# Where the token sums and six branch weights are made: out of the first projection and the SGU stage, into the two merges

## The chip, the cores and the metric

The kernel runs on one core of one Trainium2 chip. The metric is the device time of one execution in microseconds (us). Engines are named as in the profile: PE is the TensorE matmul unit (PEld its weight load), DVE the vector engine, ACT the scalar engine, POOL the GpSimd engine and SP the engine that only issues transfers. "L161" is line 161 of the kernel's file. A matrix in two parts, a high and a low half in f16, is multiplied by three f16 matmuls, which is how the kernel keeps f32 accuracy on PE.

## The reference

One layer of a hybrid token mixer is computed for 2048 sample tokens and 128 prompt tokens (`DEPTH = 1`, `D_MODEL = 1024`):

```python
xn = rmsnorm(h, ln_g) * (1 + scale) + shift
proj = einsum('btd,de->bte', xn, w_in)          # one input projection for all branches
qkv, beta, dec, z_a, u_b, v_b, z_b, x_c, z_c, gates = split(proj)
...
o_a = rmsnorm(delta_bidir(short_conv(qkv), g, beta)) * silu(z_a)     # gated DeltaNet, forward and backward
o_b = chunk_sgu(u_b, v_b, ...) * silu(z_b)                           # spatial gating
o_c = fourier_mix(x_c, grid) * silu(z_c)
pb = einsum('btnw,nwd->btnd', stack([o_a, o_b, o_c]), w_branch)
merged = einsum('btnd,btnd->btd', sigmoid(gates), pb)                # three merge gates
out = einsum('btd,de->bte', merged, w_out)
y = rmsnorm(h + gate * out)
```

The gates of the last merged branch (branch A, n = 0) need `xn` times a 1024 x 1024 block of `w_in`. For the sample tokens the kernel makes this product with seven block products in place of eight (a Strassen scheme), whose right-hand sides are sums and differences of blocks of `xn`: these are the *token sums*.

## The kernel before

The normalised tokens lie in SBUF for nearly the whole run as four f16 tiles `x00, x01, x10, x11` (first or second 1024 tokens, first or second half of the channels) in two parts each, with `xp` for the prompt tokens. The work passes through these stages, in program order:

- **Start** (to about 165 us): modulation, norm, transposes, and the z_a gates.
- **qkv** (about 165 to 490 us, L767 to L807): twelve column panels `ct` of 128 channels. A panel is five blocks of tokens (`TBS`: four of 512, one of 128); each block is 24 matmuls (8 k-slices by three parts, `gemm_T`), and ACT copies it to `raw` (L784). Then DVE runs the short convolution over the whole row of 2178 (L793 to L795), ACT a sigmoid, POOL the product (L799).
- **SGU** (about 490 to 614 us): the v projection, 17 chunks of tokens.
- u, z_b, x_c, z_c with the Fourier mixing (to about 1136 us).
- **First merge** `merge(1, ...)` (1136 to 1470) and **second merge** `merge(2, ...)` (1470 to 1807): eight column blocks `db`, each in two halves of the tokens (`HALVES`: two blocks, then three). A block is a gate product (24 matmuls), a sigmoid on ACT into an `sg` tile (L1530), a branch product (12 matmuls), and a multiplication on DVE (L1536, or L1539 with an addition on POOL, L1540).
- **Last merge** with the seven products, and the **output** projection (1807 to 2240).

Beside the panels runs a second strand of work, cut into small steps by `yield` and stepped by `pace.tick` as the panels advance: first the decay factors (`decays()`, in the qkv stage), then the preparation and the scan of the DeltaNet (`delta()`, from the SGU stage to the end of the second merge). A third strand converts weights: SP reads a block of weights into one of two `wst` tiles, ACT squares it (L209), DVE narrows the sum (`wscb`, L175), PE adds it over the partitions in one matmul with `ones`, DVE makes a power of two of it (`wsc`, L183 to L187, and `winv`, L220), ACT writes the high half (`whi`, L222) and DVE the low half (`wlo`, L223). `wlist` holds the order of all weights. Weights that are needed much later (`early`: eight blocks of `w_out`, eight of `w_branch` for branch A) are converted ahead and put into DRAM by `keep_next(i)`; each of them costs the whole chain, one factor on DVE (`oinv`, L752, or `b0inv`, L750) and two stores issued by ACT.

The token sums are a generator of 32 steps, `token_sums()` (L701): eight groups (two token halves by four k-slices) of four steps, each of which makes one 128 x 512 sum or difference, splits it into two f16 parts and stores it to DRAM (`sD`, printed as `xs`). The POOL part adds the two halves of x to an f32 tile `sg` (L717, four a group), makes one difference (L727) and one low part (L709); DVE makes three sums or differences (L723, L730, L734) and three low parts (L709); ACT makes four high parts (L708); POOL issues the four stores (L711, and L738 for the last two of all). A group holds `sg` tiles (four in all, shared with the gate sigmoids of the merges) and `st` tiles (three in all).

The order in which each engine takes its instructions is not the program's order: a scheduler replays the program with a model of durations, picks for each engine the ready instruction of the highest priority, and writes the result down. On the chip each engine then takes its list strictly in that order. `tc.high_priority()` raises an instruction in that choice; `tc.issue_after(ins)` puts instructions behind a named one.

Before the change, twelve steps of the sums are taken in the first three panels of qkv (one beside each block of 512 tokens, L786), the other twenty behind the last store of the decay factors (L804). Ten `early` weights are converted in the SGU stage (L1351), six in the second half of the qkv stage (L790).

Of the kernel before, what the change touches and what calls it, by code (L numbers as in the profile page):

```python
# [20 lines left out]
P = 128  # L21
D = 1024
KT = 8
# [88 lines left out]
def hybrid_flow_kernel(ctx: ExitStack, tc: tile.TileContext, x_prompt, x_sample, state_delta, c, c_ctx, ln_g, w_ada,  # L112
# [151 lines left out]
    wlist = []  # L264
# [4 lines left out]
    for i in range(12):  # L269
        wlist.append((w_in_[:, C_QKV + i * P:C_QKV + (i + 1) * P], KT, "w", 4))  # L270
        if i > 5:
            wlist.append(early[i - 6])
    wlist += [(w_in_[:, C_V + g * P:C_V + (g + 1) * P], KT, "v", 4) for g in range(4)] + early[6:]
    for c0 in [x_ + g * P for g in range(4) for x_ in (C_U, C_ZB)] + [x_ + g * P for g in range(4) for x_ in (C_XC, C_ZC)]:
        wlist.append((w_in_[:, c0:c0 + P], KT, "w", 4))
    gw_ = lambda n, db: w_in_[:, C_G + n * D + db * P:C_G + n * D + (db + 1) * P]
    bw_ = lambda n, db: (w_branch[0, n][:, db * P:(db + 1) * P], 4, "b", 2)
    for n in (1, 2):
        for db in range(KT):
            wlist += [(gw_(n, db), KT, "w", 4), bw_(n, db)]  # L280
    for j in range(4):
        wlist += [(gw_(0, j), KT, "w", 4), (gw_(0, 4 + j), 4, ("t2", j), 4)]
    for kind in ("t1", "t3"):
# [234 lines left out]
    for ti, (t0, tn) in enumerate(TBS):  # L518
        if t0 not in xts:
            load_x(t0, tn)  # L520
        g = 0 if t0 < NS else 1
# [235 lines left out]
    def keep_next(i):  # L757
        if 0 <= i < 8:
            keep([oD[l][:, i, :] for l in range(2)], oinv[:, i:i + 1], sx)
        elif 8 <= i < 16:  # L760
            keep([bD[l][i - 8] for l in range(2)], b0inv[:, i - 8:i - 7])
        elif i == 16:
            flush_kept()
# [7 lines left out]
    for ct in range(12):  # L771
        w = getw(1, 3 if ct < 6 else min(5, 16 - ct))
        for half in range(1):
            raw = sb(a1p, [P, LP], "raw")
            G.memset(raw[:, 0:1], 0.0)
            G.memset(raw[:, NS + 1:NS + 3], 0.0)
            G.memset(raw[:, LP - 1:LP], 0.0)
            for t0, tn in TBS:
                flip[0] ^= 1
                ps = bank(ps_d if flip[0] else ps_mm, [P, tn])  # L780
                gemm_T(ps, w, x_all(t0, tn))
                o = t0 + 1 if t0 < NS else t0 + 3
                with tc.high_priority():
                    A.activation(raw[:, o:o + tn], ps, AF.Copy, scale=w.inv)  # L784
                pace.tick(tn / 100)
                if ct < 3 and tn == 512:  # L786
                    next(sums)
                if ct > 4:
                    weight_step()
                if ct > 5 and t0 == 1024:  # L790
                    keep_next(ct - 6)
            y = sb(a1p, [P, LP - 2], "cy")
            V.tensor_scalar(y, raw[:, 0:LP - 2], convw(0, ct), None, ALU.mult)  # L793
            V.scalar_tensor_tensor(y, raw[:, 1:LP - 1], convw(1, ct), y, ALU.mult, ALU.add)
            V.scalar_tensor_tensor(y, raw[:, 2:LP], convw(2, ct), y, ALU.mult, ALU.add)  # L795
            for c0 in range(0, LP - 2, CQ):
                c1 = min(c0 + CQ, LP - 2)
                A.activation(raw[:, 1 + c0:1 + c1], y[:, c0:c1], AF.Sigmoid)  # L798
                G.tensor_tensor(y[:, c0:c1], y[:, c0:c1], raw[:, 1 + c0:1 + c1], ALU.mult)  # L799
            G.dma_start(qkvD[ct], y)  # L800
            if ct < 4 or ct > 7:
                A.activation(raw[:, 1:LP - 1], y, AF.Square, accum_out=vqs[:, ct:ct + 1])
    wsn = sb(ep, [P, WB], "st", bufs=3).rearrange("p (g q) -> p g q", g=4)
    SY.dma_start(wsn, w_spatial[0].rearrange("g p q -> p g q"))  # L804
    pace.drain()
    with tc.issue_after(dlast[0].ins):
        for _ in sums:  # L807
            pass
    a1.close()


# [517 lines left out]
    for t in range(NCH):  # L1329
# [18 lines left out]
        if t == 8:  # L1348
            SY.dma_start(cf, consts[:, _CF:_CW])
        weight_step()  # L1350
        if t % 3 != 1:  # L1351
            keep_next(6 + 2 * (t // 3) + (t % 3) // 2)
        pace.tick(5.2)
    spatial(*vprev)
    while vout:
# [147 lines left out]
    def merge(n, first, inv, each=None, halves=HALVES, mid=None, then=None):  # L1503

        steps, sinv = iter(()), None
        for db in range(KT):
# [8 lines left out]
            for h0, hn, tbs in halves:  # L1515
# [2 lines left out]
                    SY.dma_start(mrow, mD[db][:, h0:h0 + hn])  # L1518
                if each is not None and (n == 0 or db > 3):
                    next(gates, 0)  # L1520
                for t0, tn in tbs:
                    if first and db == 0:
                        for tb in TBS[0:2] if t0 == 0 else TBS[TBS.index((t0, tn)) + 1:][:1]:
# [55 lines left out]
            pace.drain()  # L1579

    inv_ = merge(2, False, inv_, finish_delta, then=(0, 17))
    cs_.close()


# [259 lines left out]
```

## Time and profile before

| what | value |
|---|---|
| median of three runs | 2239.32 us (2233.18 to 2240.04) |
| the profiled execution | 2242.02 us |
| its span, first to last instruction | 2240.2 us |
| mean granted clock of PE | 0.984 |
| PE busy | 2134.1 us, 95% of the span |
| DVE busy | 1443.1 us, 64% |
| ACT busy | 1047.8 us, 47% |
| POOL busy | 827.7 us, 37% |
| transfers | 404.94 MB, 181 GB/s on average |

The span is the profiled execution's own time without what lies around it (1.8 us). The profile gives, for each engine, its busy time, the idle time before each instruction and the event that ended it. Since every engine takes its list in order, an engine that idles before an instruction holds up everything behind it. PE is busy 95% of the span, so the time is what PE does plus the 106 us in which it does nothing, plus what it loses where its granted clock is below 1.

### The profile page before, as it was taken

How to read it: one execution, taken by the hardware profiler on the slowest of the kernel's cores; microseconds unless marked ns; L12 is line 12 of the kernel's file. 1: busy time of each engine (PE TensorE's matmuls, PEld its weight loads, DVE VectorE, ACT ScalarE, POOL GpSimd, SP SyncE). 2: the span in 40 equal slices, each digit the busy share in tenths (PEclk: the TensorE clock that was granted, in tenths of full speed). 3: DMA queues.
4: the chain of work that ended last, by engine and by line, in shares of the span. 5: the costliest groups of instructions: out<-in, count | busy, mean ns of one | idle time of the engine just before them, and what ended most of it. 6: DMA issues, size and time to landing. Idle time of an engine off the chain costs nothing. (4 is left out here: it accounts for less than half of the span.)

```text
span 2240.2 us, 42450 instructions
## 1 busy us (share of the span) xinstructions
PE 2134.1 (95%) x15878; PEld 1227.4 (55%) x15878; DVE 1443.1 (64%) x3250; ACT 1047.8 (47%) x2394; POOL 827.7 (37%) x972
## 2 busy tenths in 40 slices
PE   7998978999899999899999999999999999999998
PEld 3564433445555567788755565565555445444443
DVE  5748989558888877735565555675565455444553
ACT  3634754546565656334464444665554332222331
POOL 1445467322243332233312232345453323433443
PEclk9999989999999999999999999999999999999999
DMA  8423944448787765424475555676664856564542
GB/s 273 159 83 119 313 158 148 145 134 253 230 289 227 215 199 154 106 83 143 130 223 172 161 167 175 201 231 207 202 204 153 255 165 201 179 223 149 167 142 86
DMA packets 333625, 404.94 MB, mean 181 GB/s; under 512 B 41345, under 2 KB 240106, under 8 KB 330602
## 3 DMA queue, kind: packets, MB, share of 16 engines
q1 hardware_dynamic: 311114, 327.36, 48.1%
q0 software_dynamic: 15248, 59.66, 7.3%
q10 hardware_dynamic: 7056, 15.21, 1.8%
q8 instruction: 125, 2.05, 0.4%
q14 instruction: 82, 0.67, 0.1%
HBM read 259.83 MB, written 142.30 MB: 180 GB/s over the span
## 5 line engine op out<-in xcount | busy, mean ns | idle before, releaser
L161 PE MATMUL b<-x,whi 128*128 128x512 f16 x3008 | 908.2, 382 | 5.5 <-DVE sg L1539 2.5
L161 PE MATMUL b<-x,wlo 128*128 128x512 f16 x1504 | 574.2, 382 | 0.0
L161 PEld LDWEIGHTS <-whi 128*128 128x128 f16 x3776 | 346.5, 98 | 338.1 <-issue 35.6
L161 PEld LDWEIGHTS <-wlo 128*128 128x128 f16 x1888 | 185.6, 98 | 180.7 <-issue 13.8
L161 PE MATMUL b<-big,bhi 128*128 128x512 f16 (+1 forms) x960 | 251.7, 348 | 2.9 <-ACT big L1500 1.5
L161 PE MATMUL b<-big,blo 128*128 128x512 f16 (+1 forms) x480 | 163.4, 348 | 0.0
L161 PEld LDWEIGHTS <-x 128*128 128x128 f16 x2176 | 131.3, 98 | 43.6 <-issue 4.2
L161 PEld LDWEIGHTS <-bhi 128*128 128x128 f16 x960 | 86.8, 98 | 74.9 <-issue 3.7
L161 PE MATMUL b<-x,m 128*128 128x512 f16 x528 | 114.8, 379 | 0.0
L799 POOL TENSOR_TENSOR cy<-cy,raw 128x545 f32<-128x545 f32 (+1 forms) x48 | 72.4, 1547 | 109.6 <-ACT raw L798 109.6
L1022 POOL COPY T<-ES 32x256 f16<-32x256 f16 x68 | 31.4, 462 | 208.1 <-DMA ES<-ei 202.5
L209 ACT ACTIVATE wlo<-wst 128x1024 f16<-128x1024 f32 (+1 forms) x64 | 64.2, 1003 | 93.6 <-DMA wst<-in_w_in_dram 64.0
L223 DVE SCALAR_TENSOR_TENSOR wlo<-wst,wsc,whi 128x1024 f16<-128x1024 f32 (+1 forms) x64 | 91.1, 1426 | 19.3 <-ACT whi L222 18.8
L222 ACT ACTIVATE whi<-wst,wsc 128x1024 f16<-128x1024 f32 (+1 forms) x64 | 69.7, 1093 | 64.2 <-DVE wsc L186 57.9
L161 PE MATMUL b<-whi,x 128*128 128x128 f16 x1024 | 90.7, 219 | 0.0
L1128 POOL TENSOR_TENSOR skn<-skn,ed 128x512 f32<-128x512 f32 x34 | 36.3, 1067 | 144.8 <-DMA skn<-kv 128.5
L175 DVE CAST wscb<-wss 128x1 bf16<-128x1 f32 x101 | 15.3, 152 | 111.9 <-ACT wlo L209 74.3
L161 PE MATMUL b<-wlo,x 128*128 128x128 f16 x512 | 87.4, 219 | 0.0
L161 PEld LDWEIGHTS <-m 128*128 128x128 f16 x528 | 51.1, 98 | 61.4
L161 PE MATMUL b<-x,zhi 128*128 128x512 f16 x256 | 78.7, 383 | 0.1
L161 PE MATMUL b<-v4hi,x 128*128 128x512 f16 x256 | 78.5, 383 | 0.1
L1660 POOL TENSOR_TENSOR mrow<-mrow,sg 128x512 f32<-128x512 f32 (+1 forms) x40 | 46.5, 1165 | 82.2 <-DVE sg L1659 73.9
(483 smaller groups left out, 4475.6 us busy)
## 6 DMA issues: line engine op xcount, KB each, us to landing
wst<-in_w_in_dram SPq DMA_DIRECT2D x56, 512.0 KB, 4.7
qkv<-cy POOLq DMA_DIRECT2D x12, 1089.0 KB, 5.7
st<-br SPq DMA_DIRECT2D x48, 256.0 KB, 3.5
mrow<-mrg SPq DMA_DIRECT2D x16, 576.0 KB, 4.5
mrg<-mrow POOLq DMA_DIRECT2D x16, 576.0 KB, 3.7
dc<-dec SPq DMA_DIRECT2D x17, 512.0 KB, 4.6
kq<-qkv SPq DMA_DIRECT2D x34, 256.0 KB, 4.2
kv<-tok POOLq DMA_DIRECT2D x17, 512.0 KB, 5.6
```

What stands on the lines that cost most here:

```text
L161: PE.matmul(out, l, r, start=start, stop=stop)
L175: V.tensor_copy(sb16, ss)
L209: A.activation(w.lo, st, AF.Square, accum_out=ss)
L222: w.made = A.activation(w.hi, st, AF.Copy, scale=s)
L223: V.scalar_tensor_tensor(w.lo, st, s, w.hi, ALU.mult, ALU.subtract)
L799: G.tensor_tensor(y[:, c0:c1], y[:, c0:c1], raw[:, 1 + c0:1 + c1], ALU.mult)
L1022: G.tensor_copy(T16[rows(a0, b), :, :, b], ES[0:32, :, 2 * a0 + b, :, wT])
L1128: G.tensor_tensor(h3(kn_), h3(kn_), bc(ed[:, d, t, :], P), ALU.mult)
L1660: G.tensor_tensor(mr, mr, sg, ALU.add)
```

## The change

The sums are taken out of the qkv stage altogether. They are made in the first two merges, in the second half (`h0` not zero) of the column blocks 1 to 4: one group of four steps each time, four groups in the first merge and four in the second. Whatever is left of the generator (the last two stores) is run after the second merge.

Of the `early` weights, six (branch weights 2 to 7 of branch A) are no longer converted in the SGU stage but in the first merge, one in each of the column blocks 1 to 6, beside the second half; the seventh call there stores the last one. In the SGU stage four are left (two of `w_out`, two of `w_branch`), taken at every fourth chunk.

```diff
@@ wlist @@
-    wlist += [(w_in_[:, C_V + g * P:C_V + (g + 1) * P], KT, "v", 4) for g in range(4)] + early[6:]
+    wlist += [(w_in_[:, C_V + g * P:C_V + (g + 1) * P], KT, "v", 4) for g in range(4)] + early[6:10]
...
     for n in (1, 2):
         for db in range(KT):
-            wlist += [(gw_(n, db), KT, "w", 4), bw_(n, db)]
+            wlist += [(gw_(n, db), KT, "w", 4), bw_(n, db)] + early[9 + db:10 + db if n == 1 and db else 0]
@@ qkv stage @@
                 pace.tick(tn / 100)
-                if ct < 3 and tn == 512:
-                    next(sums)
                 if ct > 4:
                     weight_step()
...
     pace.drain()
-    with tc.issue_after(dlast[0].ins):
-        for _ in sums:
-            pass
     a1.close()
@@ SGU stage @@
         weight_step()
-        if t % 3 != 1:
-            keep_next(6 + 2 * (t // 3) + (t % 3) // 2)
+        if t % 4 == 3:
+            keep_next(6 + t // 4)
         pace.tick(5.2)
@@ merge @@
                 if each is not None and (n == 0 or db > 3):
                     next(gates, 0)
+                if h0 and db and n == 1:
+                    keep_next(9 + db)
+                if h0 and 0 < db < 5:
+                    for _ in range(4):
+                        next(sums)
                 for t0, tn in tbs:
@@ after the second merge @@
     inv_ = merge(2, False, inv_, finish_delta, then=(0, 17))
+    for _ in sums:
+        pass
     cs_.close()
```

The scheduler makes new lists of it. Three places of them follow.

**DVE, early in the qkv stage**, where the decay factors are computed (tile `tok`; L584 to L610 is one dependent chain, of which PE waits for the end). The difference of the two lists:

```order
 L598 RECIPROCAL tok_1779<-tok_1779 128x136
-L730 TENSOR_TENSOR sg_2147<-sg_2091,sg_2147 128x512
-L709 TENSOR_TENSOR st_2150<-sg_2089,st_2150 128x512
 L599 TENSOR_TENSOR tok_1779<-tok_1779 128x136
 L600 TENSOR_SCALAR tok_1779<-tok_1779 128x136
 L601 TENSOR_TENSOR tok_1779<-tok_1779 128x136
 L602 TENSOR_TENSOR tok_1779<-tok_1779 128x136
-L709 TENSOR_TENSOR st_2196<-sg_2147,st_2196 128x512
-L734 TENSOR_TENSOR sg_2243<-sg_2243,sg_2147 128x512
 L603 SCALAR_TENSOR_TENSOR tok_1779<-tok_1779 128x136
 L610 SCALAR_TENSOR_TENSOR tok_1779<-tok_1779,al_1783 128x68 x2
```

The chain keeps its order, and the sums between its links are gone.

**DVE, in the seventh panel of the qkv stage** (`ct` 6), around the narrowing `wscb` of a weight's sum of squares, for which a matmul of PE waits. Before:

```order
L223 SCALAR_TENSOR_TENSOR wlo_2917<-wst_2875,wsc_2952,whi_2916 128x1024
L730 TENSOR_TENSOR sg_4208<-sg_4201,sg_4208 128x512
L709 TENSOR_TENSOR st_4211<-sg_4199,st_4211 128x512
L734 TENSOR_TENSOR sg_4220<-sg_4220,sg_4208 128x512
L793 TENSOR_SCALAR cy_3015<-raw_2845,pc_111 128x2178
L175 CAST wscb_3062<-wss_3060 128x1
L794 SCALAR_TENSOR_TENSOR cy_3015<-raw_2845,pc_111,cy_3015 128x2178
L709 TENSOR_TENSOR st_4216<-sg_4208,st_4216 128x512
```

and now (the convolution's lines are 791 to 793 here):

```order
L220 TENSOR_TENSOR winv_2875<-wsc_2870,xsc_305 128x1
L223 SCALAR_TENSOR_TENSOR wlo_2835<-wst_2793,wsc_2870,whi_2834 128x1024
L791 TENSOR_SCALAR cy_2933<-raw_2763,pc_111 128x2178
L175 CAST wscb_2980<-wss_2978 128x1
L792 SCALAR_TENSOR_TENSOR cy_2933<-raw_2763,pc_111,cy_2933 128x2178
```

Between the low half of the weight before and the narrowing, only the first step of the convolution is left.

**POOL, in the second merge**, column block 2. Before, with the additions into `mrow`, the scan's operations (`kn`, `skn`, `T`, `R`, `o`) and the store of the row:

```order
L1022 COPY T_1513_10755<-ES_10761 32x8x32 x2
L1024 COPY R_1512_10753<-ES_10761 32x8x32 x4
L1540 TENSOR_TENSOR mrow_19318<-mrow_19318,sg_19411 128x512
L1131 TENSOR_TENSOR kn_2533_19449<-skn_19396,kn_2533_19449 128x512
L1128 TENSOR_TENSOR skn_19712<-skn_19712,ed_1399 128x512
L1203 TENSOR_TENSOR o_19493<-o_19493,of_19655 128x512
L1540 TENSOR_TENSOR mrow_19318<-mrow_19318,sg_19556 128x512
```

and now (`T` and `R` are lines 1017 and 1019, `o` is line 1198, `kn` and `skn` lines 1126 and 1123):

```order
L1123 TENSOR_TENSOR skn_19967<-skn_19967,ed_1399 128x512
L1540 TENSOR_TENSOR mrow_19904<-mrow_19904,sg_19988 128x512
L717 TENSOR_TENSOR sg_20213<-x_4_93 128x512
L717 TENSOR_TENSOR sg_20215<-x_5_94 128x512
L717 TENSOR_TENSOR sg_20222<-x_6_95 128x512
L1198 TENSOR_TENSOR o_19718<-o_19718,of_19913 128x512
L1019 COPY R_1400_10395<-ES_10403 32x8x32 x4
L727 TENSOR_TENSOR sg_20213<-sg_20222,sg_20213 128x512
L1540 TENSOR_TENSOR mrow_19904<-mrow_19904,sg_20150 128x512
L711 DMA xs_1436<-st_20218 256x1x512
L171 TENSOR_TENSOR oss_19916<-oss_19916,mhalf_91 128x4
```

A group of sums stands in pieces between the scan's operations: the first three additions, then the difference behind the scan's copies into `R`, then the first store.

## The prediction

> **What bounds the kernel now.** I read the page's first part, then the time by stage, then PE's waits, then PE's and DVE's instructions in order of time.
>
> ```profile
> PE 2134.1 (95%) x15878; PEld 1227.4 (55%) x15878; DVE 1443.1 (64%) x3250; ACT 1047.8 (47%) x2394; POOL 827.7 (37%) x972
> 165.00:490.00 325.00, 293.18 (x1590) 141.16 (x1587) 265.72 (x298) 173.46 (x253) 160.25 (x166) 0.96 0.50 168
> 490.00:614.00 124.00, 113.08 (x707) 67.85 (x706) 104.61 (x359) 72.57 (x230) 36.08 (x47) 0.99 0.77 237
> ```
>
> The last two rows are the qkv and the SGU stage: length, then busy time of PE, PEld, DVE, ACT and POOL, granted clock, transfers. PE sets the time: 2134.1 of 2240.2 us. Of the 106 us in which it idles, 31.8 (325 − 293.18) lie in the qkv stage, where DVE is busy 265.72 of 325, 82%, and 10.9 in the SGU stage (DVE 84%). What PE waits for, all over the run:
>
> ```profile
> PE b L161 <- DVE wscb L175: 24.0, 7, 8.2
> PE b L161 <- DVE tok L610: 7.1, 1, 7.1
> ```
>
> These two are the longest entries of that view: a narrowing of 128 numbers on DVE, seven times, and the end of the decay chain, once. What they cost shows best in the start of each panel's last block (five blocks a panel):
>
> ```profile
> 258.37 0.27 PE L161 MATMUL b<-xp,whi 128*128 128x128 f16 x2
> 280.45 0.28 PE L161 MATMUL b<-xp,whi 128*128 128x128 f16 x2
> 309.67 0.28 PE L161 MATMUL b<-xp,whi 128*128 128x128 f16 x2
> 346.12 0.28 PE L161 MATMUL b<-xp,whi 128*128 128x128 f16 x2
> 376.34 0.28 PE L161 MATMUL b<-xp,whi 128*128 128x128 f16 x2
> 399.75 0.28 PE L161 MATMUL b<-xp,whi 128*128 128x128 f16 x2
> 421.87 0.28 PE L161 MATMUL b<-xp,whi 128*128 128x128 f16 x2
> ```
>
> The first and the last step are 22.1 us: a panel at full speed. The four between are 29.22, 36.45, 30.22 and 23.41, together 119.30 against 4 x 22.11 = 88.4: **30.9 us** are lost here. The other place is the decay chain:
>
> ```profile
> 186.47 1.68 PE L161 MATMUL b<-tok,cst 128*128 128x68 f32 x6 [7.14 <-DVE tok L610]
> 188.79 1.06 PE L161 MATMUL b<-x,whi 128*128 128x512 f16 x2
> 189.64 0.63 PE L161 MATMUL b<-x,wlo 128*128 128x512 f16 x1
> 191.27 0.59 PE L161 MATMUL b<-x,whi 128*128 128x512 f16 x2
> 191.70 0.38 PE L161 MATMUL b<-x,wlo 128*128 128x512 f16 x1
> 290.30 0.16 PE L161 MATMUL b<-wscb,ones 128*128 128x1 bf16 x1 [3.16 <-DVE wscb L175]
> 304.47 0.16 PE L161 MATMUL b<-wscb,ones 128*128 128x1 bf16 x1 [2.04 <-DVE wscb L175]
> 325.42 0.16 PE L161 MATMUL b<-wscb,ones 128*128 128x1 bf16 x1 [8.20 <-DVE wscb L175]
> ```
>
> After 7.14 us of idling the matmuls come every 0.43 us (188.79 to 189.64, two of them), and from 191.27 on every 0.215: PE runs at half speed for about 3.4 us, which costs another 1.7. So this stop is worth 7.1 + 1.7 = **8.8 us**.
>
> [...]
>
> Now what DVE does before the longest stop, and before the end of the decay chain:
>
> ```profile
> 306.38 4.44 DVE L752 TENSOR_TENSOR oinv<-winv,xsc 128x1 f32<-128x1 f32 x1
> 321.23 1.64 DVE L734 TENSOR_TENSOR sg<-sg,sg 128x512 f32<-128x512 f32 x1
> 322.80 2.50 DVE L793 TENSOR_SCALAR cy<-raw,pc 128x2178 f32<-128x2178 f32 x1
> 325.23 0.14 DVE L175 CAST wscb<-wss 128x1 bf16<-128x1 f32 x1
> 169.57 3.50 DVE L709 TENSOR_TENSOR st<-sg,st 128x512 f16<-128x512 f32 x1
> 183.89 2.66 DVE L610 SCALAR_TENSOR_TENSOR tok<-tok,al 128x68 f32<-128x68 f32 x2
> ```
>
> The cast of 0.14 us stands behind sums (L734) and convolution (L793) in a list without a gap; and tiny operations take microseconds: 4.44 us for 128 numbers. So DVE is late for two reasons, the sums' own work and what slows its other work. The groups of DVE and POOL in 270 to 400 us, and the same DVE line in 400 to 487, where no sums run (its row stands last):
>
> ```profile
> L709 DVE TENSOR_TENSOR st<-sg,st 128x512 f16<-128x512 f32 x15 | 16.4, 1103 | 0.3 <-ACT st L708 0.3
> L730 DVE TENSOR_TENSOR sg<-sg,sg 128x512 f32<-128x512 f32 x4 | 6.1, 1518 | 0.0
> L734 DVE TENSOR_TENSOR sg<-sg,sg 128x512 f32<-128x512 f32 x4 | 5.6, 1411 | 0.0
> L723 DVE TENSOR_TENSOR sg<-sg,sg 128x512 f32<-128x512 f32 x4 | 3.7, 922 | 0.0
> L752 DVE TENSOR_TENSOR oinv<-winv,xsc 128x1 f32<-128x1 f32 x4 | 9.8, 2448 | 0.1
> L690 DVE TENSOR_TENSOR dc<-dc,cst 128x1024 f32<-128x1024 f32 x2 | 2.4, 1214 | 0.0
> L717 POOL TENSOR_TENSOR sg<-x 128x512 f32<-128x512 f16 x16 | 25.1, 1570 | 4.0 <-DVE wsc L183 2.1 <-DVE sg L730 1.9
> L711 POOL DMA_DIRECT2D xs<-st x18 | 12.7, 704 | 22.3 <-DVE st L709 9.8 <-DVE wsc L183 7.5 <-DVE wscb L175 2.1
> L752 DVE TENSOR_TENSOR oinv<-winv,xsc 128x1 f32<-128x1 f32 x3 | 1.4, 466 | 0.1
> ```
>
> The sums are 27 DVE operations here, 16.4 + 6.1 + 5.6 + 3.7 = 31.8 us, 1.18 each; beside them L752 takes 2448 ns against 466 without.
>
> **The change, part by part.**
>
> *Sums out of the qkv stage.* DVE loses those 31.8 us and at least 4 x 2.0 = 8 us of slowing out of 130. What is left is the mix that 400 to 487 us already has (two weights and a convolution a panel), and there the panels run at 22.1. In the decay chain, the sums that the new DVE list no longer has include the 3.50 at 169.57; the chain was 7.14 us late on PE. Both stops can go: −30.9 − 8.8 = **−39.7**. But not all of it. The decay factors stay: 34 operations of 128 x 1024 at 1.21 us (L690) are 41 us of DVE in the first panels, and DVE makes the weights of the next panels behind them; with PE 8.8 us earlier there, DVE may become late where it was not. From below nothing comes back; from above, 14 us: the 8.8 again and the 5.2 of the stops at 290.30 and 304.47, the first ones, where weights may be late for another reason. I take **+6**, nearer to nothing since DVE also starts the factors earlier.
>
> *Six weights out of the SGU stage.* One conversion costs DVE
>
> ```profile
> L223 DVE SCALAR_TENSOR_TENSOR wlo<-wst,wsc,whi 128x512 f16<-128x512 f32 x8 | 6.0, 745 | 0.3 <-ACT whi L222 0.3
> ```
>
> 0.745 and seven operations on 128 numbers at 0.14 (the cast at 325.23), 1.7 us; six are 10 of DVE's 104.61, which brings it from 84% to 76%. PE idles 10.9 us here; the best case is the idle share at 74% that the next fence shows (2.5%, 3 us): −8; the worst is nothing. I take **−3**, since some of the stops have other causes.
>
> *Sums and weights into the merges.* The windows are about the second half of column block 1 to the end of block 4, in the first and the second merge, and a stretch at the end of the scan:
>
> ```profile
> 1177.00:1342.00 165.00, 164.78 (x1516) 98.66 (x1514) 95.71 (x265) 73.05 (x166) 43.59 (x70) 1.00 0.55 166
> 1511.00:1676.00 165.00, 162.53 (x1465) 97.31 (x1463) 102.44 (x268) 90.37 (x261) 85.63 (x107) 1.00 0.67 205
> 1650.00:1705.00 55.00, 53.62 (x479) 32.05 (x478) 40.53 (x99) 27.54 (x76) 21.78 (x25) 1.00 0.61 191
> POOL T L1022 <- DMA ES<-ei: 132.3, 20, 18.2
> ```
>
> PE idles 0.2 and 2.5 us in the first two, 2.7 together; there is nothing to gain and everything to lose. Each window gets four groups: 24 DVE operations, which at 1.18 are 28 us (18 at the 0.745 of the row above), and four of the six conversions in the first, 7; on POOL 24 operations at up to 1.57 and 16 issues at 0.70, 49 us; 16 casts on ACT, which has half its time free. DVE goes from 58% and 62% to between 73 and 79% in both, POOL from 26% and 52% to 56% and 82%. What PE idles at such a DVE share: 2.5% at 74% (the third row), 8.8% at 84% (the SGU stage). Over 330 us that is 8 to 29 us, less the 2.7 there are: +5 to +26. If the order hides it all, 0. I take **+10**, between the third row and the SGU stage but nearer the row, which has the same scan beside the same merge.
>
> Queues: SP reads the six weights (256 KB each) between the scan's loads; POOL's issues of stores wait for DVE's or their own low halves, and behind them stand `mrow` additions and the scan's `kn`; the scan waits for those. ACT issues the twelve stores of the weights in the merge in place of the SGU stage. All of this is in the +10.
>
> [...]
>
> *Sum:* −39.7 + 6 − 3 + 10 = −26.7. From the span of 2240.2: 2213.5; with the 1.8 around it, 2215.3 for that execution. The median shown, 2239.32, is 2.7 below the profiled execution; against it the forecast is 2239.3 − 26.7 = **2213**.
>
> **The rivals.**
>
> *1. DVE stays the bound of the first panels.* For it: 41 us of decay factors and twelve convolutions stay, and DVE is at 82% over the stage. Against it: the last panels. The term +6 becomes +20, half of the gain: 2227.
>
> *2. The merges pay as the SGU stage does.* 8.8% of 330 us: +26 in place of +10: 2229. For it: POOL at 82% in the second merge, with `mrow` additions that give `sg` tiles back. Against it: three banks for matmul results, and lists written with the sums in them.
>
> *3. The scan is held up (slower).* POOL takes its list in order, and its copies into `T` wait for a transfer, 132.3 us in 20 waits, 6.6 each. If a group's additions stand behind such a wait, DVE stands at the group's first sum (L723), and behind it the scan's chain, for which PE waits. Eight groups at 6.6 are 53 us, against 36.7 gained (39.7 − 6 + 3): +16, 2256. It decides from 36.7 / 8 = 4.6 us a group on. Against it: the new list has a group's first additions ahead of such copies, and the scheduler that wrote it knows these waits.
>
> *4. The stops are not the sums'.* If the seven casts waited for ACT and for weights to land, only 8.8 + 3 would be gained and 10 paid: 2239.3 − 1.8 = 2238, no gain; the change then doesn't do what it says. For it: the stop at 290.30, the first of them. Against it: at 325.23 DVE had no gap.
>
> **How the numbers follow.** Forecast (2200 to 2222) 0.62; better than that, all stops gone and the merges free (2239.3 − 39.7 − 8 = 2192 at best), 0.07; rival 1 0.10; rival 2 0.11; rival 3 0.07; rival 4 0.03. A measurement of this kernel can tell about 0.3%, 7 us, from no change: faster is below 2232.6. Faster: 0.62 + 0.07 + 0.10 + 0.08 (most of rival 2) = 0.87; within 0.3%: 0.06 (the rest of 2, rival 4); slower: 0.07. The terms' bounds are −39.7 − 8 = −47.7 and −39.7 + 14 + 26 = +0.3; they will not all fall on one side, and with rivals 1 and 2 inside, the range is 2198 to 2232.
>
> **What would show it.** Right: every panel of qkv from the fourth on takes 22 to 23 us; PE's waits for `wscb` fall from 24.0 to under 5 and the one for `tok` from 7.1 to under 2; L752 falls below 1 us; the two merge windows show PE idle of 5 to 20 us, and DVE at 72 to 80%. Wrong: panels of 25 us and more in the first half with DVE full (rival 1); waits of PE for `sg` or for the scan's `S`, `u`, `R` of over 25 us in the merges (rival 2); DVE idle before L723 or L730 for POOL by more than 4 us a group (rival 3); `wscb` waits that stay (rival 4).

## The result, and the profile after

The change takes the time from 2239.68 to 2224.71 us (medians of four runs each, 2233.18 to 2241.46 and 2224.10 to 2225.18); the ratio is 0.9935, with a 95% interval of 0.9917 to 0.9954. That is 15 us faster. The forecast was 26.7 us (2213, range 2198 to 2232): the sign and the range hold, and 11.7 us of the gain are missing. In the profiled executions the span goes from 2240.2 to 2223.2.

The first part of the page, and the longest entries among PE's waits, of the changed kernel:

```profile
PE 2130.5 (96%) x15878; PEld 1225.3 (55%) x15878; DVE 1404.2 (63%) x3250; ACT 1043.2 (47%) x2392; POOL 836.6 (38%) x972
```

```profile
PE b L851 <- DVE n L900: 7.4, 4, 4.6
PE b L161 <- DMA ast<-in_w_ada_dram: 6.4, 5, 3.5
PE b L161 <- DVE wscb L175: 6.2, 3, 5.8
PE b L161 <- DVE X L1428: 5.7, 1, 5.7
PE b L161 <- DVE T L886: 5.4, 4, 3.5
PE b L161 <- ACT whi L222: 4.8, 2, 3.1
```

The wait for `wscb` falls from 24.0 to 6.2 and the one for `tok` (7.1) is gone. Other entries have come up: `n` and `T`, which are the preparation of the DeltaNet, and `whi`, a converted weight. `T` and `whi` lie wholly in the u/z_b stage, and so do 4.6 of the 7.4 of `n`; the forecast said nothing of that stage. Before, PE waited in that stage for DVE's `T` and for `whi` no longer than this, and for `n` not at all:

```profile
PE b L161 <- DVE T L891: 2.0, 2, 1.3
PE b L161 <- ACT whi L222: 1.2, 1, 1.2
```

The panels of the qkv stage (start of each one's last block), and the one long stop that is left there:

```profile
248.57 0.27 PE L161 MATMUL b<-xp,whi 128*128 128x128 f16 x2
270.65 0.28 PE L161 MATMUL b<-xp,whi 128*128 128x128 f16 x2
293.84 0.16 PE L161 MATMUL b<-wscb,ones 128*128 128x1 bf16 x1 [5.79 <-DVE wscb L175]
301.94 0.27 PE L161 MATMUL b<-xp,whi 128*128 128x128 f16 x2
324.31 0.28 PE L161 MATMUL b<-xp,whi 128*128 128x128 f16 x2
346.42 0.27 PE L161 MATMUL b<-xp,whi 128*128 128x128 f16 x2
368.53 0.27 PE L161 MATMUL b<-xp,whi 128*128 128x128 f16 x2
```

The four panels that took 119.3 us take 368.53 − 270.65 = 97.9: one of 31.29 and three of 22.1 to 22.4. The long one has the stop of 5.79 and, behind it, matmuls at half their rate (one in 0.43 us, up to 299.8).

For all kernels of this study I read from PE's list the start of each stage: the first matmul of the decay chain (`bdp`), of the SGU stage (`v4hi`), of the u/z_b panels, of the Fourier stage (weights as the moving side), of the gate products of its fourth and last column group, and of the output. The lengths between them, in us; the column "merges" so holds that last group of the Fourier stage too, which takes 120.0 to 120.8 in every kernel of this study (the first gate product of the first merge is at 1110.65 before and 1086.24 after):

| Kernel | decay chain and qkv | SGU | u/z_b | Fourier | merges |
|---|---|---|---|---|---|
| before | 316.8 | 130.1 | 224.1 | 168.1 | 1002.0 |
| after | 285.6 | 126.5 | 235.1 | 167.7 | 1009.9 |
| difference | −31.2 | −3.6 | **+11.0** | −0.4 | +7.9 |
| forecast | −33.7 | −3 | none | none | +10 |

The five add up to −16.3 (the span, with what lies around PE's list, to −17.0); the start before them and the output behind them do not change (151.3 and 151.2; 237.8 both). So in these two executions four of the five stages went as forecast within 2.5 us, and the whole miss is the u/z_b stage: neither its work nor its program was touched. Each length in this study is read from one execution, and executions differ: the kernels below that have this change's order of instructions in the qkv stage take 279.9 to 285.6 there. The rows of the u/z_b stage, before and after:

```profile
598.20:822.30 224.10, 211.64 (x1373) 119.35 (x1372) 184.35 (x470) 128.66 (x378) 79.05 (x98) 0.99 0.75 229
```

```profile
563.40:798.50 235.10, 215.33 (x1372) 120.12 (x1371) 184.09 (x453) 123.59 (x370) 79.67 (x100) 0.98 0.68 211
```

DVE has the same 184 us of work, POOL its 79 and ACT 5 less; PE's idle time grows from 12.5 to 19.8, and its busy time by 3.7 at a clock of 0.98 for 0.99.

The two windows of the merges that the forecast looked at, after:

```profile
1152.60:1317.60 165.00, 162.28 (x1499) 97.15 (x1498) 115.88 (x308) 83.70 (x190) 78.60 (x106) 1.00 0.64 205
1486.90:1651.90 165.00, 159.62 (x1369) 92.92 (x1367) 120.15 (x268) 91.29 (x252) 115.17 (x128) 0.99 0.66 210
```

PE idles 2.7 and 5.4 there, 5.4 more than before; another 3.0 are in the last merge, where it idled nothing before and now waits for the operands of the branch products (`big`). DVE is at 70% and 73%, POOL at 48% and 70%. The 48 operations of the sums on DVE take 0.85 us each here, not the 1.18 of the qkv stage.

### The profile page after: what moved, and what is told of

It reads as the page before. It is cut to its first block, busy times and chain, and to the rows that moved or that the text cites. A ratio compares the mean times of both kernels' runs of the same rounds, so it can differ in the third digit from the quotient of the medians.

```text
span 2223.2 us, 42450 instructions
## 1 busy us (share of the span) xinstructions
PE 2130.5 (96%) x15878; PEld 1225.3 (55%) x15878; DVE 1404.2 (63%) x3250; ACT 1043.2 (47%) x2392; POOL 836.6 (38%) x972
## 5 line engine op out<-in xcount | busy, mean ns | idle before, releaser
L797 POOL TENSOR_TENSOR cy<-cy,raw 128x545 f32<-128x545 f32 (+1 forms) x48 | 80.6, 1706 | 192.0 <-ACT raw L796 192.0
L1017 POOL COPY T<-ES 32x256 f16<-32x256 f16 x68 | 31.2, 458 | 202.7 <-DMA ES<-ei 182.4
L223 DVE SCALAR_TENSOR_TENSOR wlo<-wst,wsc,whi 128x1024 f16<-128x1024 f32 (+1 forms) x64 | 85.6, 1339 | 31.3 <-ACT whi L222 30.7
```

Source lines behind the costliest of these rows:

```text
L223: V.scalar_tensor_tensor(w.lo, st, s, w.hi, ALU.mult, ALU.subtract)
L1017: G.tensor_copy(T16[rows(a0, b), :, :, b], ES[0:32, :, 2 * a0 + b, :, wT])
```

## Experiments: which part of the change does what

The first four kernels take the change apart.

**The sums alone.** The changed kernel with its weights as before:

```diff
-    ... + early[6:10]
+    ... + early[6:]
-            wlist += [..., bw_(n, db)] + early[9 + db:10 + db if n == 1 and db else 0]
+            wlist += [..., bw_(n, db)]
-        if t % 4 == 3:
-            keep_next(6 + t // 4)
+        if t % 3 != 1:
+            keep_next(6 + 2 * (t // 3) + (t % 3) // 2)
-                if h0 and db and n == 1:
-                    keep_next(9 + db)
```

> The changed kernel with the weights as before (ten in the SGU stage, none in the merge): the sums' move alone. Theory A (the sums give the gain of the qkv stage; the u/z_b stage's 8 us came with the weights' move): qkv -31, SGU and u/z_b within 2 of before, merges +5, so 2240 - 26 = 2214. Rival B (the u/z_b stage pays because the sums left, the strand of the delta preparation being later against the panels): u/z_b +8 again, SGU 0, 2224. Rival C (it was the accident of one written order): anything between, with stops at other places than in the changed kernel.

**The weights alone.** The kernel before with those lines as in the change.

> The kernel before with the weights' move alone (four blocks beside v, six in merge 1; sums where they were). Theory A: qkv as before (panels of 29 to 36 us stay), SGU -2, u/z_b +8, merge 1 +2, so 2248. Rival B: u/z_b as before, 2240. Rival C: u/z_b between.

**No sums.** The sums' arithmetic is left out; the last merge reads x's own halves:

```diff
-                if h0 and 0 < db < 5:
-                    for _ in range(4):
-                        next(sums)
...
-    for _ in sums:
-        pass
+    for i in range(4):
+        SY.dma_start(sD[i], XQ[i % 2][i // 2])      # ahead of the second merge
```

> The changed kernel without the token sums: the four operands are filled by four transfers of x's own halves before the second merge, so the last merge computes with other numbers. It prices what the sums cost where they now are. Theory A (the sums cost the merges most of their 7 us): merges +2 against before in place of +7, so 2225 - 5 = 2220. Rival B (the merges pay for the weights, and for the order): 2224. Rival C (the sums cost more than the merges show, since the stops at the last merge's start are theirs too): 2217.

**All sums in the second merge.**

```diff
-                if h0 and 0 < db < 5:
+                if h0 and n == 2:
                     for _ in range(4):
                         next(sums)
```

> The changed kernel with all eight groups of sums in the second merge, one in each column block's second half. Theory A (the price of a merge follows DVE's share): merge 1 falls by 2, merge 2 gets 24 more DVE operations, about 28 us, which takes it to 74% or more and costs 5 to 8 more: 2225 + 4 = 2229. Rival (POOL, at 56% in merge 2, becomes the bound near 70%, its waits for the scan's transfers hold the sums up): over 2235. Rival (the order hides it): 2223.

Measured (median; ratio to the kernel before in the same session, 95% interval; then lengths of stages):

| Kernel | us | ratio | qkv | SGU | u/z_b | Fourier | merges |
|---|---|---|---|---|---|---|---|
| before | 2243.39 | | 316.8 | 130.1 | 224.1 | 168.1 | 1002.0 |
| sums alone | 2225.53 | 0.9928 (0.9914 to 0.9942) | 284.1 | 129.6 | 223.7 | 168.9 | 1021.0 |
| weights alone | 2256.33 | 1.0061 (1.0045 to 1.0077) | 317.1 | 124.6 | 233.1 | 168.5 | 1010.0 |
| no sums | 2222.59 | 0.9914 (0.9895 to 0.9933) | 287.1 | 125.0 | 235.5 | 167.7 | 1004.9 |
| all in merge 2 | 2243.41 | 0.9996 (0.9980 to 1.0012) | 281.8 | 124.5 | 233.2 | 166.6 | 1031.8 |

(The profile of the kernel before is the one already shown.) What follows:

- The gain of the qkv stage is the sums' move, all of it: −32.7 with the sums alone, +0.3 with the weights alone.
- The u/z_b stage's loss is the weights' move, all of it: 223.7 without it, 233.1 to 235.5 in the three kernels with it. Theory A held there. Alone, the weights' move makes the kernel slower: it saves 5.5 in the SGU stage and costs 9.0 in u/z_b and 8.0 in the merges.
- The sums alone give as much as the whole change (0.9928 and 0.9935): what they save in u/z_b they lose in the merges, +19 where 5 were expected. Why the merges take 1021 with the sums alone and 1010 with six weights more is not explained by any load, and it stays open: the more loaded kernel is the faster one.
- All eight groups in the second merge take the whole gain back: its merges take 30 us more than before. PE is busy 336.23 of the second merge's 360.30 us there, 24 idle, where it idled 8.2 before. I had expected 5 to 8 more. The waits are spread (in this merge 4.6 us for `S`, 3.7 for `o`, 3.6 for the gates' `sg`, 2.9 for `wscb`), not in one place.

The second merge of this kernel:

```profile
1435.20:1795.50 360.30, 336.23 (x2676) 189.95 (x2675) 244.59 (x558) 182.57 (x491) 226.88 (x242) 0.99 0.65 201
```

DVE is at 68% and POOL at 63%; the forecast's reading of what PE idles at such a DVE share (2.5% at 74%) would have given 9 us, not 24. A share of DVE does not price a merge with the scan beside it.

## Experiments: why u/z_b pays for the weights

The wait for `whi` says that a weight was late. Here is ACT's conversion of the first four weights of u/z_b (panels u0, z0, u1, z1), before and after; the first panel starts at 598.2 and at 563.4:

```profile
593.87 1.15 ACT L222 ACTIVATE whi<-wst,wsc 128x1024 f16<-128x1024 f32 x1 [0.46 <-DVE wsc L186]
610.04 1.15 ACT L222 ACTIVATE whi<-wst,wsc 128x1024 f16<-128x1024 f32 x1
617.06 1.15 ACT L222 ACTIVATE whi<-wst,wsc 128x1024 f16<-128x1024 f32 x1 [2.61 <-DVE wsc L186]
629.21 1.15 ACT L222 ACTIVATE whi<-wst,wsc 128x1024 f16<-128x1024 f32 x1 [4.30 <-DVE wsc L186]
```

```profile
515.75 1.15 ACT L222 ACTIVATE whi<-wst,wsc 128x1024 f16<-128x1024 f32 x1
544.30 1.15 ACT L222 ACTIVATE whi<-wst,wsc 128x1024 f16<-128x1024 f32 x1 [3.59 <-DVE wsc L186]
578.17 1.13 ACT L222 ACTIVATE whi<-wst,wsc 128x1024 f16<-128x1024 f32 x1
636.69 1.15 ACT L222 ACTIVATE whi<-wst,wsc 128x1024 f16<-128x1024 f32 x1 [0.36 <-DVE wsc L186]
```

Before, the fourth is there 31 us after the first panel's start. After, the first two are there 48 and 19 us ahead of it and the third 15 us behind it, all sooner than before, yet the fourth comes only 73 us behind it, when PE is through with the first two panels and waits for it (1.68 us at 637.89). Weights have four buffers (the 4 at the end of each entry of `wlist`). Who holds the fourth? The stores of the early weights tell. `keep()` puts a weight's store on a list, `kept`, and only the next `keep()` issues it, once the next weight is made:

```python
        with tc.issue_after(w.made.ins):
            flush_kept()
        kept.extend(...)
```

Before, the last early weight was followed by `keep_next(16)`, which only flushes. In the changed kernel the tenth weight is the last of the SGU stage, and the next `keep()` comes in the first merge. The store of its high half in ACT's list, and the one before it:

```profile
498.10 0.33 ACTq L767 DMA_DIRECT2D wb<-whi  x1
...
1153.39 0.33 ACTq L767 DMA_DIRECT2D wb<-whi  x1
```

So from about 498 to 1153 us one of the four buffers holds a weight that waits for its store, and the u/z_b stage runs with three. Three kernels test this.

**The store sooner**, in the changed kernel:

```diff
     spatial(*vprev)
+    flush_kept()
     while vout:
```

> The changed kernel, with the owed store of the last early weight issued at the end of the SGU stage and not at the first merge's next kept weight (654 us later). Theory A (this weight holds one of the four weight buffers all through u/z_b and Fourier, so that the fourth weight of each group of four comes late): the fourth conversion is done before the first u panel ends, the waits for whi (4.8) and for the delta preparation's T and n (10) go, u/z_b takes 224 to 226 in place of 235; 2225 - 9 = 2216, plus or minus the 8 by which the merges differ between any two written orders. Rival B (the priority of the first u weights' scales, which goes by the number of weights used so far): u/z_b stays at 233 to 235, 2225. Rival C (the delta preparation's phase): 229.

**The store later**, in the kernel before (its last `keep_next` left out of the SGU stage; in the merge, at `h0 and db == 1 and n == 1`, a `flush_kept()`):

> The kernel before, where only the owed store of the sixteenth early weight is postponed from the SGU stage to the first merge (no weight, no sum is moved). Theory A (the held buffer): u/z_b goes from 224.1 to 233 or more, 2240 + 9 = 2249. Rivals B and C (priority, phase of the preparation): u/z_b stays at 224, 2240.

**The store held**, the same with the flush tied to the merge's gate weight:

```diff
-        if t % 3 != 1:
+        if t % 3 != 1 and t < 15:
...
+                if h0 and db == 1 and n == 1:
+                    with tc.issue_after(gw.made.ins):
+                        flush_kept()
```

> The kernel before, where the owed store of the sixteenth early weight is tied to the merge's second gate weight, as in the changed kernel (in the run with the store only written later, it still went out at 597.8 us, so nothing was held). Theory A (the held buffer): the fourth weight of each group of four in u/z_b is converted after the first u panel ends, u/z_b goes from 224.1 to 232 or more, 2240 + 9 = 2249 or more. Rival B (priority or phase, which the changed kernel alters and this one does not): u/z_b stays at 224, 2240.

| Kernel | us | ratio | qkv | SGU | u/z_b | Fourier | merges |
|---|---|---|---|---|---|---|---|
| after, store sooner | 2214.13 | 0.9862 (0.9840 to 0.9885) | 281.7 | 125.6 | 223.9 | 167.4 | 1007.6 |
| before, store later in the text | 2243.54 | 0.9992 (0.9977 to 1.0007) | 322.1 | 132.5 | 224.2 | 168.4 | 1002.7 |
| before, store held | 2255.67 | 1.0044 (1.0023 to 1.0064) | 319.8 | 130.6 | 235.4 | 167.8 | 1002.9 |

The run with the store only later in the text was a miss of its own: the scheduler issued it at 597.76 all the same, since nothing tied it to the merge; nothing was held, and u/z_b did not change. Held (its last store but one is at 593.06, its last at 1150.75), u/z_b pays 11.3 us with no weight and no sum moved. Released, it pays nothing. The conversions of these two kernels, sooner and held:

```profile
511.48 1.15 ACT L222 ACTIVATE whi<-wst,wsc 128x1024 f16<-128x1024 f32 x1
539.98 1.15 ACT L222 ACTIVATE whi<-wst,wsc 128x1024 f16<-128x1024 f32 x1 [3.58 <-DVE wsc L186]
573.26 1.13 ACT L222 ACTIVATE whi<-wst,wsc 128x1024 f16<-128x1024 f32 x1
580.23 1.18 ACT L222 ACTIVATE whi<-wst,wsc 128x1024 f16<-128x1024 f32 x1
```

```profile
598.62 1.15 ACT L222 ACTIVATE whi<-wst,wsc 128x1024 f16<-128x1024 f32 x1 [0.47 <-DVE wsc L186]
613.71 1.15 ACT L222 ACTIVATE whi<-wst,wsc 128x1024 f16<-128x1024 f32 x1
620.73 1.15 ACT L222 ACTIVATE whi<-wst,wsc 128x1024 f16<-128x1024 f32 x1 [2.62 <-DVE wsc L186]
669.66 1.15 ACT L222 ACTIVATE whi<-wst,wsc 128x1024 f16<-128x1024 f32 x1 [0.41 <-DVE wsc L186]
```

With the store sooner the fourth conversion comes 7 us behind the third; with it held, 49 us. Over all fourteen profiled kernels the stage has two lengths and nothing between: 223.7 to 224.7 in the five where the store is out, 233.1 to 236.9 in the nine where it is held. So the cause is shown. What is only seen beside it: of the 11 us the waits for `whi` are 4.8, and the waits for `n` and `T`, 4.6 and 5.4 in this stage, fall to 1.7 and 2.6 with the store sooner. With conversions in bunches, DVE's list for the preparation stands differently against the panels; that this makes `n` and `T` late is read from these rows, not tested by itself.

The kernel with the store sooner is also better than both: 28.5 us less than before in its session, 0.9862 against the change's 0.9935. By these ratios that is 16 us better than the change; the u/z_b stage accounts for 11, and the rest is within the two intervals.

## Experiments: why the sums stopped PE in the qkv stage

The forecast gave two reasons, DVE's own additions (31.8 us in the late panels) and POOL's additions slowing DVE (at least 8). Two kernels put one of them alone back into the changed kernel, at the sums' places, written into a tile that nothing reads.

> The changed kernel with 40 additions of 128x512 on POOL put back into the qkv stage at the sums' old places (x's halves added into a tile that nothing reads; on top of the computation); no addition on DVE, no store, no cast on ACT. Theory A (the stops came mostly from the sums' own work on DVE): the four panels from the fifth on take 98 to 104, L752 goes up beside the additions; 2225 + 5 = 2230. Rival (the stops came from POOL's additions slowing DVE): 110 or more for the four, and the decay chain late by 5 or more: 2240.

> The changed kernel with 56 additions of 128x512 on DVE put back at the sums' old places (into a tile that nothing reads; on top of the computation); none on POOL, no store. Theory A (DVE's own work): the four panels from the fifth on take 108 to 120 in place of 97.9, the wait for wscb is back at 15 or more, 2225 + 15 = 2240. Rival (POOL's additions did it): under 102, 2227.

The edit, in both (the same calls of `next(dums)` in the first three panels, and the rest tied to the last decay factor; a second operation on the tile follows in one step of four on POOL, in three of four on DVE):

```diff
+        t_ = sb(a1p, [P, 512], "dm", bufs=2)
+        G.tensor_tensor(t_, h_, l_, ALU.add)        # V in the other kernel
...
+                if ct < 3 and tn == 512:
+                    next(dums)
```

With no data to wait for, all of them ran beside the decay chain, between 154 and 201 us; so these two kernels say nothing of the late panels, and much of the chain. POOL's alone (2232.60 us, ratio 0.9958, 0.9939 to 0.9977) bring its stop back whole: from the chain's first matmul to the end of the second panel it is 62.2 us, 62.9 before and 53.2 after. DVE's alone (2236.82, 0.9968, 0.9953 to 0.9984) do not, 48.7, though DVE is busy 33.66 of the 34 us there. They cost later: the next three panels take 85.8 in place of 66.3, with stops of 6.1 us for the copy to `raw` and 4.3 for `wscb`. Over the whole qkv stage the two cost about the same, 294.3 with POOL's and 295.8 with DVE's against 285.6. The chain itself is no faster with DVE's additions: its last operation on DVE ends at 186.0, with POOL's at 184.4, without either at 174.8. What differs is PE's list. Ahead of the matmul that needs the chain stand 1101 matmuls in the changed kernel and with POOL's additions, 1161 with DVE's, and 1113 in the kernel before: the scheduler put 60 more of panel work there for DVE's additions, and none for POOL's slowing. The chain's operations on DVE, in the changed kernel, then with POOL's additions alone:

```profile
171.82 1.00 DVE L598 RECIPROCAL tok<-tok 128x136 f32<-128x136 f32 x1
172.86 0.30 DVE L599 TENSOR_TENSOR tok<-tok 128x136 f32<-128x136 f32 x1
173.19 0.23 DVE L600 TENSOR_SCALAR tok<-tok 128x136 f32<-128x136 f32 x1
173.45 0.30 DVE L601 TENSOR_TENSOR tok<-tok 128x136 f32<-128x136 f32 x1
177.36 0.30 DVE L618 COPY tok<-b 128x136 f32<-128x136 f32 x1 [2.53 <-PE b L161]
```

```profile
175.54 1.00 DVE L598 RECIPROCAL tok<-tok 128x136 f32<-128x136 f32 x1
176.58 1.09 DVE L599 TENSOR_TENSOR tok<-tok 128x136 f32<-128x136 f32 x1
177.71 1.06 DVE L600 TENSOR_SCALAR tok<-tok 128x136 f32<-128x136 f32 x1
178.81 1.14 DVE L601 TENSOR_TENSOR tok<-tok 128x136 f32<-128x136 f32 x1
185.72 0.30 DVE L618 COPY tok<-b 128x136 f32<-128x136 f32 x1 [1.34 <-PE b L161]
```

An operation of 0.23 or 0.30 us takes about as long as one of POOL's additions beside it (1.14 in the mean of the 40), while the reciprocal and the copy out of the matmul's bank keep their 1.00 and 0.30. Not every other operation is held: L597 at 175.28 and L624 at 186.40, one-input operations like L600 (1.06 in place of 0.23), keep their 0.23. How POOL's additions hold DVE up, and what decides which of its operations they hold, these rows do not show.

For the late panels, two more kernels make the additions read the panel's own result, one after each block of the fifth to the eighth panel:

```diff
                 pace.tick(tn / 100)
+                if 3 < ct < 8 and tn == 512:
+                    t_ = sb(a1p, [P, 512], "dm", bufs=2)
+                    G.tensor_tensor(t_, raw[:, o:o + tn], raw[:, o:o + tn], ALU.add)   # V, and a second one behind 3 of 4, in the other
```

> The changed kernel with 16 additions of 128x512 on POOL (of a panel's own result, into a tile that nothing reads; on top of the computation), one behind each block of the fifth to the eighth panel, where the kernel before had 16 of the sums' there. The four panels took 97.9 in the changed kernel and 93.6 to 99.3 with the same work in other orders, 119.3 before. Theory A (there the stops are the sums' own work on DVE): 94 to 102. Rival (POOL's additions hold DVE up there too, as in the decay chain): 106 or more, and DVE's operations on 128 numbers above 1 us.

> The changed kernel with 28 additions of 128x512 on DVE at the same places (the kernel before had 27 of the sums' there), none on POOL. Theory A (own work): 28 by 0.68 = 19 us more in DVE's list, the four panels take 106 to 116, waits for wscb of 8 or more. Rival (it takes POOL beside them): 94 to 102.

Neither brings the stops back: the four panels take 98.8 with POOL's 16 additions and 96.3 with DVE's 28, against 97.9 (2227.52 and 2227.63 us, ratios 0.9928 and 0.9932, as the change itself). Neither alone is the cause there, the forecast's "own work" included. DVE's groups say where the time was. The same lines of the list, before (280.4 to 399.8), after (270.6 to 368.5), and with DVE's additions alone (270.9 to 367.1); operations, busy us, mean ns:

```profile
280.40:399.80 119.40, 95.76 (x490) 44.70 (x489) 110.45 (x112) 59.56 (x93) 80.40 (x87) 0.91 0.46 156
...
L223 DVE SCALAR_TENSOR_TENSOR wlo<-wst,wsc,whi 128x1024 f16<-128x1024 f32 x10 | 21.5, 2148 | 3.5 <-ACT whi L222 3.4
L220 DVE TENSOR_TENSOR winv<-wsc,xsc 128x1 f32<-128x1 f32 x9 | 12.3, 1362 | 0.3
```

```profile
270.60:368.50 97.90, 91.85 (x489) 43.81 (x488) 54.02 (x84) 47.23 (x73) 32.39 (x42) 0.97 0.42 139
...
L223 DVE SCALAR_TENSOR_TENSOR wlo<-wst,wsc,whi 128x1024 f16<-128x1024 f32 x10 | 15.5, 1546 | 18.3 <-ACT whi L222 18.3
L220 DVE TENSOR_TENSOR winv<-wsc,xsc 128x1 f32<-128x1 f32 x9 | 1.8, 195 | 0.3
L752 DVE TENSOR_TENSOR oinv<-winv,xsc 128x1 f32<-128x1 f32 x4 | 0.6, 160 | 0.1
```

```profile
270.90:367.10 96.20, 90.23 (x489) 43.35 (x488) 76.10 (x110) 45.83 (x70) 32.56 (x40) 0.98 0.38 130
```

DVE goes from 54.0 to 76.1 with its own additions alone, and to 60.6 with POOL's alone: together 29 us more. Before the change it was 56 more. Some 29 of those are not additions but the same old operations, slower: 6.0 in `wlo`, 10.5 in `winv`, 9.2 in `oinv` (L752: 2448 ns against 160, four times), 3 in the convolution's first line (2138 ns against 1353, four times). The sums' own 27 operations were slowed too: 1.18 us each, against 0.80 for the 28 of the kernel with DVE's additions alone. POOL had 80 us of work there, not 54 as with its 16 additions alone: the sums' low halves and the issues of their stores came on top. So what the late panels had before is a DVE at 92%, a good part of it slowing; with DVE's additions alone it is at 79%, with POOL's 16 alone at 61%, and has room. That the lists allow for work and not for slowing, as at the chain, would fit, but it is argued here and not tested: the two together were not run, and how much of the stops comes from which stays open.

## Experiment: the sums spread

The kernel with the store sooner, with one step of the sums before each block in place of four at once:

```diff
-                if h0 and 0 < db < 5:
-                    for _ in range(4):
-                        next(sums)
                 for t0, tn in tbs:
+                    if 0 < db < 5 and tn == 512:
+                        next(sums)
```

> The changed kernel with the store sooner (2214 us) and the sums spread: one step before each block of 512 tokens of column blocks 1 to 4 in both merges, in place of four steps at once in each second half. Theory A (the merges pay for DVE's bursts): the part from the merges' start to the output, 1007.6 in that kernel and 1001.9 before the change, falls by 3 to 5: 2210. Rival (what is left there, 5.7, is the accident of a written order): within 8 of 2214 on either side. Rival (steps spread hold the sg tiles longer): 2222.

2216.12 us, ratio 0.9878 (0.9856 to 0.9899), not told apart from 0.9862; its merges take 1012.1, not less than 1007.6. That bursts are what the merges pay for is not borne out; the 4.5 us between the two kernels are no more than executions differ by.

How much that is, the kernels of this study tell by the way. Six have the merges' code exactly as in the change (after, store sooner, and the four with additions in the qkv stage): 1009.9, 1007.6, 1010.2, 1012.7, 1015.2, 1010.6, mean 1011.0. Three have it as before, up to one store: 1002.0, 1002.7, 1002.9. So moving eight groups and six weights in costs 1011.0 − 1002.5 = 8.5 us. The expectations above took such differences for the accident of a written order. The traces say otherwise: five of the six (all but the one with the store sooner) have the same instructions in the same order on every engine there, and still differ by 5.3 us, 1009.9 to 1015.2. In the qkv stage five kernels with one order (after, sums alone, all in merge 2, store sooner, spread) take 279.9 to 285.6, mean 282.6, and four with the order of before (before, weights alone, store later, store held) 316.8 to 322.1, mean 319.0. What differs from one execution to the next is not looked into here.

## Why the prediction was right, and where it failed

The measured 2224.71 lies in the range, but outside the 2200 to 2222 that had the chance of 0.62. It is nearest to rival 1's 2227, and that is chance: but for one panel, DVE did not bound the first panels.

- **The sums out of the qkv stage, −39.7.** Right in size: both stops were the sums'. The decay chain's part, forecast −8.8, is 53.2 − 62.9 = −9.7 (the half rate behind the stop of 7.14 lasts 4.7 us, not 3.4: the granted clock before is 0.50 from 186.5 to 191.1, of which the 128x512 matmuls have 3.3, 187.94 to 191.27); the four panels' part, forecast −30.9 less the residual, is −21.4 in these two executions, and −26.8 between the means of the four and the five executions with one order. But the reason for the late panels was mis-sized: the slowing of DVE's other work was put at "at least 8 us" and is 29, and the sums' own work on DVE alone stops PE neither at the chain nor in the four late panels (in the three between, it does). The forecast took time on DVE for the cause without asking which of it the lists already allow for.
- **The residual, +6.** 97.9 − 88.4 = 9.5 us stay in this execution, nearly all in one panel of 31.29 behind the stop of 5.79. It was named with its place (weights of the first panels). The five executions with this order take 92.3 to 97.9 there, mean 94.5: 6.1 in the mean, so right.
- **Six weights out of the SGU stage, −3.** 126.5 − 130.1 = −3.6. Over ten kernels with four weights the mean is 125.7, over four with ten 130.7: −5.0.
- **Sums and weights into the merges, +10.** +7.9, and 8.5 as a mean of six; in the two windows themselves PE idles 5.4 more, and 3.0 are in the last merge, for which nothing was forecast. The size came from DVE's share, and that reading is not sound: the kernel with all sums in the second merge idles almost three times what it says.
- **What failed** is the sentence "ACT issues the twelve stores of the weights in the merge in place of the SGU stage", and "all of this is in the +10". It counted the stores' issue and not what an owed store holds. Fourteen stores are issued there, not twelve: the first two are those of the last weight that stays in the SGU stage, and they moved behind the u/z_b and the Fourier stage with that weight's buffer. The sum had no term for u/z_b: it should have been +11.0. With it the sum would be −15.7; −15.0 was measured. That the two meet so closely is in part luck, since single stages differ by 5 us and more between executions.
- **The signs named.** The waits for `tok` (gone) and L752 (160 ns) came as named, and PE's idle time in the two windows, 8.1 us in all; the waits for `wscb` (6.2) are just over their 5, DVE in the first window (70%) just under its 72, and one panel takes 31.29 and not 22 to 23.
- **The rivals.** DVE as the bound of the first panels (2227): no, but for one panel. The merges paying 26 (2229): no. The scan held up by POOL (2256): no for the change as it is, in which DVE waits 1.2 us in all for POOL at the groups' sums; with all groups in one merge the merges pay 30, near that price, but spread over the scan's waits and not at the place that rival named. The stops not being the sums': no; without the sums' move the qkv stage takes 317.1.

## What to carry to other kernels

When a store is issued by the next call and not by its own, moving the next call moves the buffer's release: for each step that a change moves, ask not only what it issues but what it had set free, and find the next allocation of that pool. An operation that waits in another stage shows as a late weight in a stage that nobody touched, so the forecast should have a line for every stage between the old place and the new. At the decay chain the list made room for work that the scheduler knew of and none for slowing that it didn't know of, so ask which of an engine's time the lists already allow for; the work itself was paid for in the three panels behind (19.6 us). A stage's price from an engine's busy share is a guess. And the same order of the same instructions differed by 5.3 us in the merges and 5.7 in the qkv stage from one execution to another, so a term of that size is not read from one profile.

## What the runs showed of the hardware

- Beside POOL's additions of 1.14 us in the mean, most of the chain's operations of 0.23 or 0.30 on DVE take 1.06 to 1.14; where POOL also makes low halves and issues stores, operations on 128 numbers of 0.16 and 0.20 take 2.45 and 1.36 in the mean. A reciprocal (1.00) and a copy out of a matmul's bank (0.30) keep their time. I had put this slowing at a side effect of 8 us; it was 29 of the 56 us that DVE got rid of in the late panels. The 4.44 us of L752 at 306.38 outlast any one instruction of POOL there: an issue, an addition, two products and another issue (306.1 to 310.9, the longest 1.3).
- DVE at 99% (33.66 of 34 us) beside the decay chain did not stop PE there, though the three panels behind it took 19.6 us longer; DVE at 49% (16.54 of 34) with POOL's slowing did, for 4.75 us and 9.0 in all. What stopped PE at the chain was the delay for which the list had left no room.
- After the stop of 3.16 us before the change (290.30) the granted clock is 0.50 up to 293.5 and a 128x512 matmul comes every 0.43 us; after the one of 2.04 (304.47) it is 1.00 and they come every 0.215 from the first on. So the panel of 29.22 lost 5.2 us to its stops and about 1.7 to the clock.
